# mLSTM products on full 128x128 arrays with zeroed halves, and a block inverse that starts from 8x8 blocks

## The chip, the cores and the metric

The kernel runs on one core of a Trainium2 chip. One core has a matmul engine (PE, with its weight loads listed as PEld), VectorE (DVE), ScalarE (ACT), GpSimd (POOL) and the engine that issues the transfers (SP), each with its own instruction queue, worked off in the order in which the program writes it. The metric is the time of one execution on the device, in microseconds, as the median of several runs.

## What is computed

One inference step through two layers, for a prompt of 1024 tokens and, with the same weights, for 8 sample tokens that each bring their own states. The first layer has eight heads of gated DeltaNet beside eight heads of mLSTM, the second has GLA beside retention. All matrices are float32. Two pieces of the first layer matter here, and the kernel works on both in 8 chunks of L = 128 tokens for each head.

```python
# gated DeltaNet, per head and chunk (k, q, v: L x 128; S: 128 x 128)
A = where(tri_strict, decay * (k @ k.T), 0) * beta[:, None]
rhs = beta[:, None] * (v - gam * (k @ S))
U = triangular_solve(A + eye, rhs, lower=True, unit_diagonal=True)
o = gam * (q @ S) + ((q @ k.T) * decay) @ U
S = exp(last) * S + (k * exp(last - bh)).T @ U

# mLSTM, per head and chunk (q, k: L x 64; v: L x 128; C: 64 x 128, n: 64)
num = s0[:, None] * (q @ C) + P @ v
den = s0 * (q @ n) + P.sum(-1)
h = num / maximum(abs(den), exp(-m_t))[:, None]
C = se * C + (k * we).T @ v
n = se * n + k.T @ we
```

## The kernel before

The program does not run as it is written. A recorder (class `Recorder`) collects every operation with what it reads and writes, estimates its duration, and then lists the operations of each engine in an order of its own: a backward pass gives each operation a priority by the work that depends on it, a forward pass hands each engine the ready operation of the highest priority. All instructions of the trace therefore carry the line number of the one call that replays them, L452. The planner's costs matter to the order alone. For a transfer of up to 256 KB it takes 450 ns, its bytes at 40 per ns where rows are shorter than 128 bytes, and 1400 ns until the landing: 2.7 us for 32 KB in 32-byte rows. A change in the program moves instructions everywhere, since the planner then finds another order.

Buffers that take part in the order are single slots with a name (`s_N`, `s_EM`, `s_Y`, `s_aT`, `s_vs`, `s_kd`, `s_va`, `s_mp`, `s_qs`, `s_kwe` in the trace), three each of `tmp` and `pt`, two buffers `wf` for the weights as they are loaded and two each of `whi` and `wlo`, their upper and lower parts, which ScalarE and VectorE split for the projections. A projection `pj` is 72 matmuls of 128x128 weights on 344 columns: 8 blocks of the input, 3 column groups, three products each (`whi` twice, `wlo` once). Products of the mixers go to PSUM banks A (gated DeltaNet) and B (mLSTM). Small buffers and constants show as `arena` and `base`.

`even` runs the first layer: it sets up, then alternates for each gated DeltaNet head `gdn_proj` and `gdn_mix` with a few steps of the generator `mlstm_heads`, so that projections, the inverse and both scans can be mixed by the planner.

`gdn_mix` makes `N`, the strictly lower triangular 128x128 matrix of each of the 8 chunks, stored transposed (1024 columns), and calls `inverse(N)` for the inverse of I plus that matrix. `inverse` treats the 8 chunks and the four 32x32 diagonal blocks together. It starts at pairs: four masked copies (`masked`, with the integer map `icode`) and four subtractions give `D`, the inverses of the 2x2 diagonal blocks; `Dt` is `D` transposed within the 32x32 blocks. Four doubling steps then go from 2 to 4, 8, 16 and 32. Each has 32 matmuls of 32x32 (8 chunks x 4 blocks) of N with Dt, a masked copy on VectorE, 32 matmuls of that with D, a subtraction and a transpose. The two last levels (32 to 64 to 128) use larger products and the small buffer `iw`, on which GpSimd prepares a transposed copy `Yt`. `Y` is the result. After it the scan of `gdn_mix` goes over the chunks with the state S: products with k, qg, Y, kd and aT in turn, each waiting for an update on VectorE or ScalarE.

`mlstm_mix` scans one mLSTM head. Two heads share the 128 partitions: the even head x = 0 has rows 0 to 63 (`hp`), the odd head the others. Per chunk there are three products: P with va (128x130: v, a column of ones for the normaliser, and one of padding), `qs` with the state C from the second chunk on, and `kwe` with va for the update of C. The second uses 64 rows of the array and the third writes 64 columns, by `tile_position`:

```python
self.mm(po[:, i, :], P[:, c, :], va[:, c, :], start=True, stop=C is None)
self.mm(po[:, i, :], self.qs[hp, s], C[hp, :], start=False, stop=True, tile_position=(b0, 0))
self.mm(pc[hp, 0:130], self.kwe[:, c, x, :], va[:, c, :], tile_position=(0, b0))
V.scalar_tensor_tensor(Cn[hp, :], C[hp, :], self.g_se[hp, p, c:c + 1], pc[hp, 0:130], ...)
```

Of the kernel before, what the change touches and what calls it, by code (L numbers as in the profile page):

```python
# [9 lines left out]
F32 = mybir.dt.float32  # L10
F32R = mybir.dt.float32r
AF = mybir.ActivationFunctionType
ALU = mybir.AluOpType
# [4 lines left out]
T = 1024  # L18
NS = 8
W = T + NS  # L20
# [4 lines left out]
NC = T // L  # L25
# [14 lines left out]
def host_constants():  # L40
    f = np.float32
    c = {}
# [7 lines left out]
    s, t = np.arange(L)[:, None], np.arange(L)[None, :]  # L50
# [7 lines left out]
    lm = np.zeros((32, 6, 32), f)  # L58
    ss, tt = np.arange(32)[:, None], np.arange(32)[None, :]
# [5 lines left out]

    code = np.zeros((32, 32), f)
    code[lm[:, 4, :] > 0] = 1.0
    for i, m in enumerate((2, 4, 8, 16)):
        code[lm[:, 3 - i, :].T > 0] = 2.0 + i
    c["icode"] = np.tile(code, (4, 1))  # L70

# [396 lines left out]
class Step:  # L468
# [537 lines left out]
    def even_gates(self, ps):  # L1006
        nc, a = self.nc, self.a
        dma = nc.sync.dma_start
# [79 lines left out]
        ss = self.slot("Y", [128, 6, NS], name="gss")  # L1088
# [9 lines left out]
        self.act(ss[96:104, 3, :], ss[96:104, 3, :], AF.Exp, scale=-1.0)  # L1098
        for i, r in enumerate((ss[0:8, 0, :], beta[32:40, T:W], ss[96:104, 5, :], ss[96:104, 4, :], ss[96:104, 3, :])):
            dma(self.ed[3 + i], r)  # L1100
# [193 lines left out]
    def inverse(self, N):  # L1294

        V, G = self.nc.vector, self.nc.gpsimd

        t = self.slot("EM", name="inv")
        D, Dt, At, qt = (t[:, 256 * i:256 * i + 256].rearrange("p (c t) -> p c t", c=NC) for i in range(4))

        def masked(E, out, x, i, b=slice(0, 128)):
            code = self.icode[b].unsqueeze(1).to_broadcast([b.stop - b.start, NC, 32])
            E.scalar_tensor_tensor(out, code, float(i), x, op0=ALU.is_equal, op1=ALU.mult)

        blocks = [slice(32 * j, 32 * j + 32) for j in range(4)]
        for j, b in enumerate(blocks):
            masked(V, At[b], N[b, :, b], 1, b)
        for b in blocks:
            V.tensor_tensor(D[b], self.ident[b, b].unsqueeze(1).to_broadcast([32, NC, 32]), At[b], op=ALU.subtract)
        V.transpose(Dt, D)  # L1310
        for i in range(2, 6):
            p = self.ps(None, [128, NC, 32])
            for c in range(NC):
                for j, b in enumerate(blocks):
                    self.mm(p[b, c, :], N[b, c, b], Dt[b, c, :], tile_position=(32 * j, 32 * j))
            masked(V, At, p, i)
            p = self.ps(None, [128, NC, 32])
            for c in range(NC):
                for j, b in enumerate(blocks):
                    self.mm(p[b, c, :], At[b, c, :], D[b, c, :], tile_position=(32 * j, 32 * j))  # L1320
            V.tensor_tensor(D, D, p, op=ALU.subtract)
            V.transpose(Dt, D)
# [11 lines left out]
        iw = self.small([128, 512], "iw", bufs=1)  # L1334
# [13 lines left out]
        iy = iw[:, 0:512].rearrange("p (c t) -> p c t", c=NC)  # L1348
# [119 lines left out]
    def mlstm_mix(self, h, v):  # L1468
# [33 lines left out]
        for n in (3, 3, 2):  # L1502
            po = self.ps(None, [128, 3, 130], 0)
            c0 = c
            for i in range(n):
                s = slice(128 * c, 128 * c + 128)
                self.mm(po[:, i, :], P[:, c, :], va[:, c, :], start=True, stop=C is None)
                if C is not None:
                    self.mm(po[:, i, :], self.qs[hp, s], C[hp, :], start=False, stop=True, tile_position=(b0, 0))
                pc = self.ps(i=1)  # L1510
                self.mm(pc[hp, 0:130], self.kwe[:, c, x, :], va[:, c, :], tile_position=(0, b0))
                Cn = self.small([128, 130], "C", bufs=2)
# [100 lines left out]
    def even_setup(self):  # L1613
# [3 lines left out]
        self.icode = self.const([128, 16], "icode").bitcast(mybir.dt.bfloat16)  # L1617
        code = self.slot("EM", [128, 32], name="code")
# [4 lines left out]
        self.nms = self.const([128, 2, 2, NS], "mnms")  # L1623
        self.qq = self.const([128, 2, 2, NS], "mqq")
# [480 lines left out]
    def build(self):  # L2105
        tc, nc = self.tc, self.nc
        with ExitStack() as ctx:
# [22 lines left out]
            self.rd = [dr.tile([4, QB], F32, name=f"rd{i}") for i in range(2)]  # L2130
            self.program()
# [105 lines left out]
```

## Time and profile before

| | |
|---|---|
| time before, median of 3 runs | 2360.61 us (2356.93 to 2366.92) |
| the profiled execution, its own time | 2372.93 us |
| its span | 2371.2 us |
| mean granted clock of PE | 0.979 |
| busy: PE, PEld, DVE, ACT, POOL | 97%, 89%, 60%, 32%, 22% |
| PE matmul records | 20892 |

The page describes one execution, which took 12.3 us longer than the median of the runs. Times in the rows are microseconds, except the mean of one instruction, which is in ns. A row of a group reads: line, engine, operation, output from inputs with the shapes, how often; then busy time and mean of one; then the idle time of the engine just before them and what ended it. A matmul that reads float32 shows as two records. Sizes such as 64*128 are rows times columns of the array in use. In the rows of the timeline the first number is the start, the second the length; consecutive records of one kind are put together, so the distance from one row's start to the next is what the row took of the engine.

### The profile page before, as it was taken

What the parts mean: (1) busy time and instruction counts of PE and PEld (TensorE: products, weight loads), DVE (VectorE), ACT (ScalarE), POOL (GpSimd) and SP (SyncE); (2) the same over time, 40 slices, a digit from 0 to 9 for tenths busy, and PEclk for the clock granted to TensorE, in tenths of its full rate; (3) what the DMA queues carried; (4) which work ended last, traced back from release to release, by engine and by line L of the source; (5) the groups of instructions that cost most, each with busy time, mean ns of one, the idle gap of its engine ahead of it and who ended that gap; (6) DMA issues with size and microseconds to landing.
All of it is one profiled execution on the core that took longest, in us unless ns stands there. A gap on an engine that the chain in (4) does not pass through costs nothing.

```text
span 2371.2 us, 48673 instructions
## 1 busy us (share of the span) xinstructions
PE 2297.3 (97%) x20892; PEld 2113.3 (89%) x20892; DVE 1411.5 (60%) x2700; ACT 747.3 (32%) x1374; POOL 518.8 (22%) x374
## 2 busy tenths in 40 slices
PE   7989999999999999999999999999999999998998
PEld 5878788798998989989898999999999999998998
DVE  6764645556374564755544326767877877878332
ACT  4323222232322223232233114323423423435322
POOL 4122111111202112030122003141341341343100
PEclk8999998999998999999999999999999999999999
DMA  9451533322222322222146222124224233246222
GB/s 268 117 146 53 159 102 113 108 83 71 72 55 70 91 64 78 64 88 73 56 145 173 90 63 72 46 82 127 66 87 124 63 92 119 63 126 219 81 63 90
DMA packets 250990, 232.54 MB, mean 98 GB/s; under 512 B 13595, under 2 KB 223253, under 8 KB 250766
## 3 DMA queue, kind: packets, MB, share of 16 engines
q1 hardware_dynamic: 250774, 229.42, 32.4%
q8 instruction: 164, 2.69, 0.5%
q14 instruction: 52, 0.43, 0.1%
HBM read 184.25 MB, written 45.33 MB: 97 GB/s over the span
## 4 chain that ended last, share of the span: by engine, by line
PE 86%; DVE 4%; DMA 2%; issue 1%; ACT 1%; POOL 0%; SPq 0%; POOLq 0%; DVEq 0%; ACTq 0%
PE pj L452 65%; PE A L452 14%; PE B L452 6%; DMA s_pt<-yd 1%; DVE s_h L452 1%; DVE arena L452 1%; DVE wlo L452 1%; DVE s_N L452 1%; DMA wf<-in_ev_w_in 1%; DMA s_tmp<-sd 0%; DVE s_tmp L452 0%; DVE s_vs L452 0%; DVE s_zz L452 0%; ACT whi L452 0%; DMA sd<-s_mp 0%
## 5 line engine op out<-in xcount | busy, mean ns | idle before, releaser
L452 PE MATMUL pj<-s_h,whi 128*128 128x344 f32 (+1 forms) x6024 | 1505.9, 328 | 6.3 <-DVE s_h L452 4.0
L452 PEld LDWEIGHTS pj<-s_h,whi 128*128 128x128 f32 (+1 forms) x6024 | 1049.9, 190 | 41.2 <-issue 25.0
L452 PE MATMUL pj<-s_h,wlo 128*128 128x344 f32 (+1 forms) x3024 | 986.4, 327 | 0.3 <-DVE wlo L452 0.3
L452 PEld LDWEIGHTS pj<-s_h,wlo 128*128 128x128 f32 (+1 forms) x3024 | 573.0, 190 | 20.8 <-issue 16.8
L452 DVE TENSOR_TENSOR wlo<-wf,whi 128x1024 fp32r<-128x1024 f32 (+1 forms) x144 | 199.2, 1383 | 262.1 <-ACT whi L452 248.5
L452 ACT ACTIVATE whi<-wf 128x1024 fp32r<-128x1024 f32 (+1 forms) x146 | 152.1, 1042 | 339.1 <-PE pj L452 280.8
L452 ACT ACTIVATE s_pt<-pj 128x344 f32<-128x344 f32 (+1 forms) x170 | 77.0, 453 | 340.1 <-PE pj L452 329.6
L452 POOL TENSOR_TENSOR arena<-arena,base 128x8 f32<-128x8 f32 (+5 forms) x38 | 59.5, 1566 | 471.7 <-DVE arena L452 471.5
L452 POOL TENSOR_TENSOR s_tmp<-s_EM 128x512 f32<-128x512 f32 (+1 forms) x60 | 84.2, 1426 | 157.9 <-PE A L452 62.0
L452 ACT ACTIVATE s_u<-pj 128x344 f32<-128x344 f32 x93 | 41.6, 452 | 162.5 <-PE pj L452 98.5
L452 DVE SCALAR_TENSOR_TENSOR s_pt<-s_u,base,s_pt 128x1024 f32<-128x1024 f32 x72 | 92.2, 1280 | 0.4
L452 DVE SCALAR_TENSOR_TENSOR arena<-arena,A 128x128 f32<-128x128 f32 (+1 forms) x84 | 32.8, 390 | 86.2 <-PE A L452 85.9
L452 DVE STREAM_TRANSPOSE s_kd<-s_u 32x256 f32<-32x256 f32 x128 | 55.8, 436 | 23.8 <-ACT s_u L452 21.4
L452 DVE SCALAR_TENSOR_TENSOR s_zz<-s_pt,pj 128x344 f32<-128x344 f32 x96 | 48.7, 509 | 29.1 <-ACT s_pt L452 28.2
L452 POOL TENSOR_TENSOR s_tmp<-s_tmp,arena 128x1024 f32<-128x1024 f32 (+2 forms) x26 | 44.5, 1721 | 94.6 <-PE A L452 69.5
L452 DVE SCALAR_TENSOR_TENSOR arena<-arena,B 64x130 f32<-64x130 f32 (+1 forms) x84 | 31.3, 372 | 56.8 <-PE B L452 56.2
L452 ACT ACTIVATE arena<-A,arena 128x128 f32<-128x128 f32 x64 | 23.5, 367 | 121.7 <-PE A L452 121.7
L452 ACT ACTIVATE s_tmp<-s_tmp 128x1024 f32<-128x1024 f32 (+1 forms) x44 | 46.1, 1057 | 40.6 <-POOL s_tmp L452 29.3
L452 POOL TENSOR_TENSOR s_kd<-s_kd,s_vs 128x1032 f32<-128x1032 f32 x8 | 20.2, 2524 | 172.8 <-ACT s_vs L452 172.8
L452 DVE STREAM_TRANSPOSE s_vs<-s_v 32x256 f32<-32x256 f32 x128 | 55.8, 436 | 1.9
L452 ACT ACT_TABLE_LOAD x41 | 52.6, 1283 | 5.1 <-DMA s_h<-in_x_prompt 4.4
L452 POOL MEMSET s_u<- 128x3 f32 x24 | 2.4, 100 | 233.6 <-DVE s_pt L452 233.6
(644 smaller groups left out, 3689.5 us busy)
## 6 DMA issues: line engine op xcount, KB each, us to landing
wf<-in_ev_w_in SPq DMA_DIRECT2D x64, 512.0 KB
wf<-in_od_w_in SPq DMA_DIRECT2D x48, 512.0 KB
wf<-in_ada_w SPq DMA_DIRECT2D x32, 512.0 KB
s_pt<-yd SPq DMA_DIRECT2D x24, 516.0 KB
s_tmp<-sd SPq DMA_DIRECT2D x24, 512.0 KB
yd<-s_qg SPq DMA_DIRECT2D x15, 516.0 KB
wf<-in_ev_w_out SPq DMA_DIRECT2D x14, 512.0 KB
wf<-in_od_w_out SPq DMA_DIRECT2D x14, 512.0 KB
```

The source lines that it names most:

```text
L452: op.fn(*[self.placed(x) for x in op.args], **{k: self.placed(x) for k, x in op.kw.items()})
```

## The change

Two parts. In `mlstm_mix` the product with qs uses all 128 rows: the state buffers C are now constants `mC` (two for each parity of the head) whose other half is zeroed once in `even_setup`, so the rows of the other head add nothing. The product with kwe uses both heads' 128 columns, and only the own half of the result is read.

In `inverse` the levels 1 to 8 are replaced. The four columns of 32x32 diagonal blocks of N go to DRAM (`nd`, four transfers with rows of 128 bytes); a read back puts each of the 8 x 4 x 4 = 128 diagonal blocks of 8x8 on a partition of its own (`n8`, 1024 rows of 32 bytes). Seven steps of substitution, two VectorE operations each on at most 128x7x7 elements, give the inverses `y8`. They go to DRAM (`yd`, whose other elements were zeroed at the start) and four transfers bring 32x32 blocks back as `D`. Two doubling steps remain, 8 to 16 and 16 to 32. The buffer `iw` is gone: `Yt` uses the slot of `D`, `At`, `qt` and `Dt`, so GpSimd's memset and copies for it come after the second correction's matmuls. `even_setup` gets the loads and memsets for the constants, and one small buffer gets a seventh row so that an activation doesn't write in place.

```diff
     code = np.zeros((32, 32), f)
-    code[lm[:, 4, :] > 0] = 1.0
-    for i, m in enumerate((2, 4, 8, 16)):
-        code[lm[:, 3 - i, :].T > 0] = 2.0 + i
+    for i in range(2):
+        code[lm[:, 1 - i, :].T > 0] = 1.0 + i
     c["icode"] = np.tile(code, (4, 1))
+    c["i8"] = np.tile(np.eye(8, dtype=f).reshape(1, 64), (128, 1))
...
     def inverse(self, N):
-        t = self.slot("EM", name="inv")
-        D, Dt, At, qt = (t[:, 256 * i:256 * i + 256].rearrange("p (c t) -> p c t", c=NC) for i in range(4))
...
+        nd, yd = (self.nyd[x][self.turn(x, 2)] for x in ("nd", "yd"))
+        by32 = lambda x, j: x.rearrange("(c j q) x -> c j (q x)", c=NC, j=4)[:, j, 0:1024].rearrange(
+            "c (s t) -> s c t", t=32)
+        by8 = lambda x: x[:, 0:256].rearrange("m (r t) -> m r t", t=32)[:, :, 0:8]
         blocks = [slice(32 * j, 32 * j + 32) for j in range(4)]
         for j, b in enumerate(blocks):
-            masked(V, At[b], N[b, :, b], 1, b)
-        for b in blocks:
-            V.tensor_tensor(D[b], self.ident[b, b].unsqueeze(1).to_broadcast([32, NC, 32]), At[b], op=ALU.subtract)
+            dma(by32(nd, j), N[b, :, b])
+        n8, y8, t8 = (self.const([128, 8, 8], x) for x in ("n8", "y8", "t8"))
+        dma(n8, by8(nd))
+        G.tensor_copy(y8, self.i8)
+        for s in range(7):
+            n = 7 - s
+            V.tensor_tensor(t8[:, 0:s + 1, 0:n], y8[:, 0:s + 1, s:s + 1].to_broadcast([128, s + 1, n]),
+                            n8[:, s:s + 1, s + 1:8].to_broadcast([128, s + 1, n]), op=ALU.mult)
+            V.tensor_tensor(y8[:, 0:s + 1, s + 1:8], y8[:, 0:s + 1, s + 1:8], t8[:, 0:s + 1, 0:n], op=ALU.subtract)
+        dma(by8(yd), y8)
+
+        t = self.slot("EM", name="inv")
+        D, At, qt, Dt = (t[:, 256 * i:256 * i + 256].rearrange("p (c t) -> p c t", c=NC) for i in range(4))
+        for j, b in enumerate(blocks):
+            dma(D[b], by32(yd, j))
         V.transpose(Dt, D)
-        for i in range(2, 6):
+        for i in range(1, 3):
...
-        iw = self.small([128, 512], "iw", bufs=1)
...
-        iy = iw[:, 0:512].rearrange("p (c t) -> p c t", c=NC)
+        iy = t[:, 0:512].rearrange("p (c t) -> p c t", c=NC)
...
                 if C is not None:
-                    self.mm(po[:, i, :], self.qs[hp, s], C[hp, :], start=False, stop=True, tile_position=(b0, 0))
+                    self.mm(po[:, i, :], self.qs[:, s], C, start=False, stop=True)
                 pc = self.ps(i=1)
-                self.mm(pc[hp, 0:130], self.kwe[:, c, x, :], va[:, c, :], tile_position=(0, b0))
-                Cn = self.small([128, 130], "C", bufs=2)
+                self.mm(pc[:, 0:130], self.kwe[:, c].rearrange("p x d -> p (x d)"), va[:, c, :])
+                Cn = self.mC[:, 2 * x + self.turn(f"C{x}", 2), :]
...
+        self.i8 = self.c_load("i8", [128, 8, 8])
+        zero = self.slot("aT", [128, 264], name="zero")
+        G.memset(zero, 0.0)
+        for x in self.nyd["yd"]:
+            self.nc.sync.dma_start(x, zero)
...
+        self.mC = self.const([128, 4, 130], "C")
+        for x in range(2):
+            G.memset(self.mC[64 - 64 * x:128 - 64 * x, 2 * x:2 * x + 2, :], 0.0)
...
+            self.nyd = {x: [dr.tile([128, 264], F32, name=f"{x}{i}") for i in range(2)] for x in ("nd", "yd")}
```

What the planner makes of it, at three places. A row is line, operation, output from inputs, and how often it stands there in a row.

PE at the inverse of the fifth gated DeltaNet head, before. The products of `s_EM` with `s_N` and of `s_EM` alone are the two batches of a doubling step; `s_mq` with `s_mk` belongs to mLSTM, `pj` to the projections:

```order
L452 MATMUL A_115<-s_EM_69,s_N_70 32x32 x32
L452 MATMUL B_117<-base,s_pt_83 128x128 x3
L452 MATMUL B_116<-s_mq_73,s_mk_74 128x128 x2
L452 MATMUL A_113<-s_EM_69 32x32 x32
L452 MATMUL B_116<-s_mq_73,s_mk_74 128x128 x2
L452 MATMUL B_117<-s_mq_73,s_mk_74 128x128 x3
L452 MATMUL A_114<-s_EM_69,s_N_70 32x32 x32
```

The same head after the change:

```order
L451 MATMUL A_113<-s_EM_69,s_N_70 32x32 x32
L451 MATMUL B_117<-arena,base 128x16
L451 MATMUL B_116<-s_va_75,s_mp_78 128x130
L451 MATMUL A_114<-s_EM_69 32x32 x32
L451 MATMUL B_117<-s_va_75,s_kwe_76 128x130
L451 MATMUL B_116<-s_va_75,s_mp_78 128x130
L451 MATMUL pj_110<-s_h_442,wlo_108 128x344
L451 MATMUL pj_110<-s_h_450,whi_106 128x344
L451 MATMUL pj_110<-s_h_461,whi_106 128x344
```

A batch is still 32 products, but the mLSTM products of P and va now stand between them, and there are four such batches instead of eight. Between the last product of q and k of a head and its first batch the new order has 126 to 168 projection matmuls, the old one 48 or 49.

PE where the two scans alternate, before; `arena` with `s_qs` is the product of qs with C, `s_va` with `s_kwe` the update:

```order
L452 MATMUL B_116<-arena,s_qs_77 128x130
L452 MATMUL A_115<-arena,s_k_63 128x128
L452 MATMUL A_113<-s_qg_68,arena 128x128
L452 MATMUL B_117<-s_va_75,s_kwe_76 64x130
L452 MATMUL A_115<-arena,s_Y_72 128x128
L452 MATMUL B_116<-s_va_75,s_mp_78 128x130
```

And after:

```order
L451 MATMUL A_113<-s_aT_71,arena 128x128
L451 MATMUL B_117<-s_va_75,s_kwe_76 128x130
L451 MATMUL B_116<-s_va_75,s_mp_78 128x130
L451 MATMUL A_115<-arena,s_k_63 128x128
L451 MATMUL A_113<-s_qg_68,arena 128x128
L451 MATMUL B_116<-arena,s_qs_77 128x130
L451 MATMUL B_117<-s_va_75,s_kwe_76 128x130
L451 MATMUL A_115<-arena,s_Y_72 128x128
```

The mix of the scans is much the same; kwe's output is 128x130 instead of 64x130.

SP, in the fifth head, after the change. `nd` and `yd` are the new DRAM buffers, `arena` is n8 and then y8; `sd` and `in_state_gdn` belong to the sample tokens, `wf` are weights:

```order
L451 DMA nd_129<-s_N_70 32x8x32
L451 DMA wf_104<-in_ev_w_in 128x8x128
L451 DMA nd_129<-s_N_70 32x8x32 x2
L451 DMA sd_125<-s_tmp_85 8x128
L451 DMA nd_129<-s_N_70 32x8x32
L451 DMA s_tmp_86<-sd_125 128x1024
L451 DMA s_tmp_85<-in_state_gdn 128x8x128
L451 DMA arena<-nd_129 128x8x8
L451 DMA wf_105<-in_ev_w_in 128x8x128
L451 DMA out_s_gdn<-s_tmp_87 128x8x128
L451 DMA yd_131<-arena 128x8x8
L451 DMA s_EM_69<-yd_131 32x8x32 x4
```

Before, the same stretch had the loads of `sd`, of `in_state_gdn` and of the weights alone:

```order
L452 DMA sd_125<-s_tmp_85 8x128
L452 DMA s_tmp_86<-sd_125 128x1024
L452 DMA s_tmp_85<-in_state_gdn 128x8x128
L452 DMA out_s_gdn<-s_tmp_87 128x8x128
L452 DMA wf_105<-in_ev_w_in 128x8x128
```

Ten transfers are put between them, and a weight load now stands behind the load of the 8x8 blocks, another behind the store of their inverses. On VectorE the fourteen substitution operations of that head stand between seven updates of the sample states (`s_tmp` from `s_tmp` and `s_k`, 128x128 each), and a weight split follows them:

```order
L451 SCALAR_TENSOR_TENSOR s_tmp_85<-s_tmp_87,s_k_63,s_tmp_85 128x128
L451 TENSOR_TENSOR arena<-arena 128x4x4
L451 TENSOR_TENSOR arena<-arena 128x5x3 x2
L451 TENSOR_TENSOR arena<-arena 128x6x2 x2
L451 TENSOR_TENSOR arena<-arena 128x7 x2
L451 TENSOR_TENSOR wlo_109<-wf_105,whi_107 128x1024
```

Before the change no VectorE operation in `inverse` waited for a transfer.

More of the change, by code (lines that the diff above doesn't have):

```diff
@@ L1086, in even_gates @@
         dma(self.ed[2], mp[0:8, 2, :])
-        ss = self.slot("Y", [128, 6, NS], name="gss")
+        ss = self.slot("Y", [128, 7, NS], name="gss")
         nc.gpsimd.memset(ss, 0.0)
@@ L1097, in even_gates @@
         self.act(ss[96:104, 4:6, :], ss[96:104, 4:6, :], AF.Exp)
-        self.act(ss[96:104, 3, :], ss[96:104, 3, :], AF.Exp, scale=-1.0)
-        for i, r in enumerate((ss[0:8, 0, :], beta[32:40, T:W], ss[96:104, 5, :], ss[96:104, 4, :], ss[96:104, 3, :])):
+        self.act(ss[96:104, 6, :], ss[96:104, 3, :], AF.Exp, scale=-1.0)
+        for i, r in enumerate((ss[0:8, 0, :], beta[32:40, T:W], ss[96:104, 5, :], ss[96:104, 4, :], ss[96:104, 6, :])):
             dma(self.ed[3 + i], r)
@@ L1294, in inverse @@
     def inverse(self, N):
-        V, G = self.nc.vector, self.nc.gpsimd
-        t = self.slot("EM", name="inv")
-        D, Dt, At, qt = (t[:, 256 * i:256 * i + 256].rearrange("p (c t) -> p c t", c=NC) for i in range(4))
-        def masked(E, out, x, i, b=slice(0, 128)):
-            code = self.icode[b].unsqueeze(1).to_broadcast([b.stop - b.start, NC, 32])
-            E.scalar_tensor_tensor(out, code, float(i), x, op0=ALU.is_equal, op1=ALU.mult)
+        V, G, dma = self.nc.vector, self.nc.gpsimd, self.nc.sync.dma_start
+        nd, yd = (self.nyd[x][self.turn(x, 2)] for x in ("nd", "yd"))
+        by32 = lambda x, j: x.rearrange("(c j q) x -> c j (q x)", c=NC, j=4)[:, j, 0:1024].rearrange(
+            "c (s t) -> s c t", t=32)
+        by8 = lambda x: x[:, 0:256].rearrange("m (r t) -> m r t", t=32)[:, :, 0:8]
         blocks = [slice(32 * j, 32 * j + 32) for j in range(4)]
         for j, b in enumerate(blocks):
-            masked(V, At[b], N[b, :, b], 1, b)
-        for b in blocks:
-            V.tensor_tensor(D[b], self.ident[b, b].unsqueeze(1).to_broadcast([32, NC, 32]), At[b], op=ALU.subtract)
+            dma(by32(nd, j), N[b, :, b])
[12 more added lines that the diff above has]
+            dma(D[b], by32(yd, j))
         V.transpose(Dt, D)
-        for i in range(2, 6):
+        for i in range(1, 3):
             p = self.ps(None, [128, NC, 32])
@@ L1315, in inverse @@
                     self.mm(p[b, c, :], N[b, c, b], Dt[b, c, :], tile_position=(32 * j, 32 * j))
-            masked(V, At, p, i)
+            V.scalar_tensor_tensor(At, self.icode.unsqueeze(1).to_broadcast([128, NC, 32]), float(i), p,
+                                   op0=ALU.is_equal, op1=ALU.mult)
             p = self.ps(None, [128, NC, 32])
```

## The prediction

> **What bounds the kernel now.** I read the page's busy times first, then its chain that ended last, then the windows of the first layer, then the groups on the matmul engine.
>
> ```profile
> span 2371.2 us, 48673 instructions
> ...
> PE 2297.3 (97%) x20892; PEld 2113.3 (89%) x20892; DVE 1411.5 (60%) x2700; ACT 747.3 (32%) x1374; POOL 518.8 (22%) x374
> ...
> PE 86%; DVE 4%; DMA 2%; issue 1%; ACT 1%; POOL 0%; SPq 0%; POOLq 0%; DVEq 0%; ACTq 0%
> ```
>
> PE is busy 97% of the span and is 86% of the chain that set the end; VectorE (DVE) is busy 60%. Work taken from PE shortens the kernel, and work added elsewhere costs only where PE comes to wait for it. Both edits lie in the first layer, from 160 to 1310 us:
>
> ```profile
> 160.00:1310.00 1150.00, 1121.11 (x11407) 999.90 (x11396) 623.62 (x1323) 319.36 (x650) 209.32 (x154) 0.97 0.31 91
> ```
>
> The columns are length, then busy time of PE, PEld, DVE, ACT and POOL, then granted clock, DMA share and GB/s. PE is bound here as well: 1121 of 1150 us, at a mean clock of 0.97. The groups that the change touches:
>
> ```profile
> L452 PE MATMUL A<-s_EM 32*32 32x32 f32 x2432 | 33.4, 195 | 9.3 <-issue 9.2
> L452 PE MATMUL A<-s_EM,s_N 32*32 32x32 f32 x2304 | 30.9, 194 | 6.7 <-issue 6.7
> ...
> L452 PE MATMUL B<-s_va,s_kwe 128*64 128x130 f32 x128 | 30.5, 323 | 0.2 <-DVE arena L452 0.2
> L452 PE MATMUL B<-arena,s_qs 64*128 64x130 f32 x112 | 29.1, 343 | 1.4 <-DVE arena L452 1.4
> ```
>
> An f32 matmul is two records (passes): 56 products of qs with the state and 64 updates from kwe. Records overlap, so their durations don't add; I use distances between starts.
>
> **Part A, the mLSTM products on full arrays.** A stretch where the two scans alternate (start, us):
>
> ```profile
> 749.56 0.49 PE L452 MATMUL B<-arena,s_qs 64*128 64x130 f32 x2
> 750.02 0.49 PE L452 MATMUL A<-arena,s_k 128*128 128x128 f32 x2
> 750.34 0.39 PE L452 MATMUL A<-s_qg,arena 128*128 128x128 f32 x2
> 750.66 0.43 PE L452 MATMUL B<-s_va,s_kwe 128*64 128x130 f32 x2
> 751.02 0.49 PE L452 MATMUL A<-arena,s_Y 128*128 128x128 f32 x2
> 751.35 0.39 PE L452 MATMUL B<-s_va,s_mp 128*128 128x130 f32 x2
> 751.67 0.49 PE L452 MATMUL B<-arena,s_qs 64*128 64x130 f32 x2
> ```
>
> And a run of full-array products:
>
> ```profile
> 692.24 0.39 PE L452 MATMUL A<-s_k 128*128 128x128 f32 x2
> 692.46 0.39 PE L452 MATMUL A<-s_q,s_k 128*128 128x128 f32 x2
> ...
> 692.91 0.39 PE L452 MATMUL A<-s_q,s_k 128*128 128x128 f32 x2
> ```
>
> Full products of one shape start 0.22 us apart. In the scan qs takes 0.46, kwe 0.36, and each full product beside them 0.32: the price sits at the change of shape, on both sides. From 749.56 to 751.67 six products take 2.11 us instead of 6 x 0.22 = 1.34, so 0.77 a chunk. At 56 chunks with both products that is 43 us, plus 8 first chunks with kwe alone at 0.14: 44, the upper bound. The lower bound keeps the neighbours at 0.32 and lets only their own slots go: 56 x (0.46-0.22) + 64 x (0.36-0.22) = 22. I take **-40**, near the upper one, because in the quoted stretch every full product borders a changed shape; a tenth is left for chunks whose neighbours are something else. That full arrays make the passes themselves no longer is seen at mp: the same 130 columns on the full array, 0.32 in the same place.
>
> The Trainium skill, "TensorEngine Tiling (Array Packing)", section "The Problem", counts a contraction of 64 or less among the cases where the full array is wasted, and the change goes the other way. Its section "Key Properties" also says that a switch of tiling mode drains the array. The trace bears out the second (0.46 against 0.22) and not the first. By the first alone this part would give 0.
>
> **Part B, the inverse's matmuls.** One batch is 32 products of 32x32, 64 records:
>
> ```profile
> 714.41 0.32 PE L452 MATMUL pj<-s_h,wlo 128*128 128x344 f32 x1
> 714.57 0.32 PE L452 MATMUL pj<-s_h,whi 128*128 128x344 f32 x1
> 714.82 0.75 PE L452 MATMUL A<-s_EM,s_N 32*32 32x32 f32 x64
> 715.50 0.42 PE L452 MATMUL pj<-s_h,whi 128*128 128x344 f32 x1
> 715.76 0.32 PE L452 MATMUL pj<-s_h,wlo 128*128 128x344 f32 x1
> ```
>
> From 714.57 to 715.76 lie two projection matmuls at 0.16 (714.41 to 714.57) and one batch: 1.19 - 0.32 = 0.87. The doubling steps go from four to two, two batches each, in eight heads: 32 batches, **-28**. By the batch's own slot alone (714.82 to 715.50) it is 0.68 x 32 = 22, the lower bound; a doubling batch next to other changed shapes might give up to 34.
>
> **Part C, idle inside these batches.** The two groups of 32x32 products sit idle 9.3 + 6.7 = 16 us, nearly all "issue". Ten batches a head use these arrays, four go: 16 x 0.4, **-6** (bounds 0 and -10).
>
> **Part D, what is added.** The start of the inverse becomes a chain through DRAM: four stores of N's diagonal blocks, a load as 8x8 blocks, 14 small DVE operations, a store, four loads, a transpose. Rows nearest to its steps:
>
> ```profile
> L452 DVE SCALAR_TENSOR_TENSOR s_N<-A,arena,s_EM x64: 335/343/351, 145.3 to 1127.4; 128x128 f32<-128x128 f32 x64
> ...
> L452 DVE STREAM_TRANSPOSE s_EM<-s_EM x40: 429/445/448, 157.1 to 1154.4; 128x256 f32<-128x256 f32 x40
> ...
> L452 DVE SCALAR_TENSOR_TENSOR s_EM<-arena,s_N x32: 361/421/1767, 152.4 to 1131.9; 32x256 f32<-32x256 bf16 x32
> L452 DVE TENSOR_TENSOR s_EM<-base,s_EM x32: 405/416/422, 155.1 to 1133.8; 32x256 f32<-32x256 f32 x32
> ```
>
> ```profile
> L452 DVE TENSOR_TENSOR arena<-arena 128x8 f32<-128x8 f32 x56 | 9.8, 175 | 7.7 <-ACT arena L452 6.8
> ```
>
> ```profile
> 1265.73 12.36 DMA s_pt<-yd
> ...
> 2194.67 1.61 DMA rd<-s_aT
> 2196.33 3.79 DMA s_aT<-rd
> ```
>
> ```profile
> 746.80 0.33 SPq L452 DMA_DIRECT2D yd<-arena  x1
> ```
>
> N's eight products take 8 x 0.34 = 2.7, about 4 with the pieces that feed them. Four stores: 4 x 0.33 to issue and 1.61 until the last has landed, 2.9. The load: 0.33 + 3.79 = 4.1. The 14 operations: 14 x 0.175 = 2.5, with seven state updates of 128x128 for the sample tokens set between them at 0.34, 4.9. Store 1.9, four loads 1.3 + 3.8 = 5.1, transpose 0.4. Together **about 23 us**. These legs have short rows that no row shows: I take them from the small store (1.61) and the read-back (3.79); the ends are nothing and the 12.36 us that one read-back of 516 KB held up the chain.
>
> The cover: before, 9.65 us pass from the last product of q and k (692.91) to the first batch:
>
> ```profile
> 702.31 0.32 PE L452 MATMUL pj<-s_h,wlo 128*128 128x344 f32 x1
> 702.56 0.75 PE L452 MATMUL A<-s_EM,s_N 32*32 32x32 f32 x64
> ```
>
> The new order puts 126 to 168 projection matmuls there where 48 stood: at 0.16, 20 to 27 us, and some 5 us of scan products. So 25 us or more cover 23, just.
>
> DVE itself gains per head: it loses eight operations of 0.42 and two doubling steps' three of 0.42 to 0.45, and adds 14 x 0.175: 3.4 + 2.6 - 2.5 = 3.5 us less, which its 60% hides. SP issues ten more DMAs a head, 3.3 us; weight loads queue behind those that wait, but two buffers of 72 matmuls (11.5 us each) stand ahead. The reuse of EM moves GpSimd's steps behind the second correction:
>
> ```profile
> L452 POOL COPY arena<-s_EM 32x256 f32<-32x256 f32 x16 | 6.5, 409 | 192.8 <-DVE s_EM L452 192.4
> ...
> L452 POOL MEMSET arena<- 32x256 f32 x8 | 2.4, 302 | 24.3 <-PE A L452 24.3
> ```
>
> 0.3 + 2 x 0.41 = 1.1 us later; the projection matmuls between those batches hide it, else it costs 9 us over eight heads. The planner allows about 2.7 us for a small leg; a leg of 3.79 is 1.1 later, and behind the DVE operation that waits for it stands a weight split (wlo), and then the transpose, for which PE waits: 8 x 1.1, **+10** with the extra setup (bounds 0 and the rivals).
>
> **Sum**, against the profiled execution's own 2372.9 us: 2372.9 - 40 - 28 - 6 + 10 = 2309. That execution lies 12.3 above the median of the runs (2360.6), so **2297 us**.
>
> **Rivals.**
>
> Slow legs: each leg takes what the longer loads do in the chain:
>
> ```profile
> 357.81 6.93 DMA s_tmp<-sd
> ```
>
> That is 4.2 us past the planner's 2.7, and after a stop PE runs at half clock for a while:
>
> ```profile
> 709.88 0.59 PE L452 MATMUL A<-s_EM 32*32 32x32 f32 x46 [1.54 <-issue]
> ...
> 713.01 0.49 PE L452 MATMUL pj<-s_h,wlo 128*128 128x344 f32 x1
> 713.30 0.49 PE L452 MATMUL pj<-s_h,whi 128*128 128x344 f32 x1
> ```
>
> Starts 0.29 apart instead of 0.16, from 710.4 to 713.9: 1.6 us lost. So 8 x (4.2 + 1.6) = 46 in place of 10, **2333**. For it: cover and chain are near equal, and the load of the 8x8 blocks is issued behind two loads of 512 KB. The Trainium skill, "DMA: Bandwidth & Descriptors", section "Specifications", says that below 512 B a transfer does a read-modify-write and misses line rate, and the rows here are 32 and 128 B; no run here shows its price. Against it: a leg moves only 32 to 128 KB.
>
> No gain from shape: the scan's products are slow for their 130 columns or for waits on DVE, and stay so. Part A falls away: **2337**. For it: the groups of qs and kwe wait for DVE at times. Against it: the k products, with 128 columns, slow down beside them and run at 0.22 elsewhere.
>
> The chain of the recurrence: PE gets through a chunk faster than DVE updates the state, and half of A comes back as waits: **2317**.
>
> More than counted: stops of 1.54 us like the one above lie in the batches that go, about 16 x 0.4 / 1.54 = 4, each with 1.6 us of half clock, and A gives all 44, B 34: **2280**.
>
> **Slower**: the first substitution operation stands at the head of DVE until the 8x8 blocks have landed; behind it stand the other substitution steps and the next weight split, and PE stops at the first product of that split. With a leg of 12.36, 9.7 past the plan: 8 x (9.7 + 1.6) = 90, so 2373 - 74 + 90 - 12 = **2377**. It outweighs the gain of 74 from 9.2 a head, a leg of 10.3 us; a whole projection's matmuls ahead of that split (11.5 us) would take its edge off. For it: each engine takes its work in the written order. Against it: that row is one wait of 516 KB after a layer's end.
>
> **How the numbers follow.** Forecast 0.46, slow legs 0.19, no gain from shape 0.08, recurrence 0.10, more than counted 0.12, slower 0.05. About 0.5% (12 us) is what a measurement can tell from no change: faster means under 2349. Of the slow legs and the lost A a quarter could end within it, and a little of the rest: faster 0.89, same 0.06, slower 0.05. The range reaches from 2262 (all upper bounds, some more half clock gone) to 2340, past slow legs and the lost A.
>
> **What would show it.** In the scan, products of qs and kwe start 0.22 apart and their neighbours too; 32x32 records fall from 4736 to 2688; no idle on PE before the first batch; the clock of 160 to 1310 us is no lower than 0.97. Idle of PE before the first batch or before wlo's matmuls, ending after a small load lands, would make the prediction wrong; so would starts of 0.32 that stay.

## The result and the profile after

| | before | after |
|---|---|---|
| median | 2358.77 us (4 runs, 2355.56 to 2366.92) | 2287.93 us (4 runs, 2282.23 to 2290.45) |
| ratio, 95% interval | | 0.9691, 0.966 to 0.9723 |
| profiled execution: own time, span | 2372.93, 2371.2 us | 2289.05, 2287.0 us |
| mean granted clock of PE | 0.979 | 0.987 |

The changed kernel takes 3.1% less time. The forecast was 2297 us with a range of 2262 to 2340. The page of the changed kernel, busy times and then shares of the chain that ended last:

```profile
span 2287.0 us, 44726 instructions
...
PE 2221.4 (97%) x18844; PEld 2070.0 (91%) x18844; DVE 1382.8 (60%) x2700; ACT 747.7 (33%) x1374; POOL 527.7 (23%) x385
...
PE 88%; DMA 4%; DVE 4%; issue 1%; ACT 1%; POOL 1%; SPq 1%; POOLq 0%; DVEq 0%; ACTq 0%
```

PE still sets the time: 97% busy, with 2048 records fewer, the 32 batches of 64. The first layer, in the windows view of the changed kernel (columns as before):

```profile
160.00:1228.00 1068.00, 1053.67 (x9535) 967.79 (x9534) 594.25 (x1338) 322.70 (x653) 213.01 (x162) 0.99 0.36 102
```

It takes 1068 us where it took 1150: 82 of the 84 us between the two profiled executions. PE's busy time there falls by 67 us, its idle time from 29 to 14, and its clock rises from 0.97 to 0.99. What PE waited for in the first layer, in the waits view, engine and releaser, then us in all, times and the longest, first of before:

```profile
PE A L452 <- issue: 15.9, 10, 3.0
```

and of the changed kernel:

```profile
PE A L451 <- issue: 1.9, 3, 0.8
...
PE A L451 <- DVE s_EM L451: 1.0, 2, 0.9
```

The stops inside the 32x32 batches are nearly gone, and the new wait, for the transpose behind the way through DRAM, is 1 us over all eight heads. The array shapes in the group rows of the changed kernel:

```profile
L451 PE MATMUL B<-s_va,s_kwe 128*128 128x130 f32 x128 | 26.0, 284 | 0.1
...
L451 PE MATMUL A<-s_EM 32*32 32x32 f32 x1408 | 19.9, 194 | 0.1
L451 PE MATMUL B<-arena,s_qs 128*128 128x130 f32 x112 | 22.9, 286 | 0.4 <-DVE arena L451 0.4
```

qs took 343 ns a record and kwe 323; both are at 285 now, on the full array.

**How the runs are read below.** A difference of medians mixes three things: the time that PE works, the time that it stands, and the time that it loses at half clock. They can be told apart from numbers of one profiled execution: span minus busy time is what PE stands; span x (1 - mean clock) is what it loses (the clock of stopped stretches counted in); busy time minus that is the **net work**, PE's work at full clock. For before: 2371.2 - 2297.3 = 73.9, 2371.2 x 0.021 = 49.8, net 2247.5. After: 65.6, 29.7, net 2191.7. So of 84 us, 56 are work that is gone, and 28 are stops and half clock. The clock has three places, so the last two columns below are good to about 1 us. They also describe one execution each: over 40 executions of the kernel before, the clock ran from 0.973 to 0.989 and the span from 2349.9 to 2385.1 us, with the same order.

| kernel | median us | ratio to before (95%) | span | PE stands | lost to clock | net work |
|---|---|---|---|---|---|---|
| before | 2358.8 to 2365.3, in five measurements | | 2371.2 | 73.9 | 49.8 | 2247.5 |
| before, planner 185 ns | 2362.9 | 0.9986 (0.996 to 1.0012) | 2352.5 | 73.3 | 37.6 | 2241.6 |
| before, planner overlap | 2353.7 | 0.9958 (0.9923 to 0.9992) | 2351.1 | 75.0 | 28.2 | 2247.9 |
| slot reuse alone | 2341.4 | 0.9908 (0.9881 to 0.9934) | 2337.7 | 61.2 | 28.1 | 2248.4 |
| slot reuse, qs full | 2335.9 | 0.9874 (0.9847 to 0.9902) | 2333.7 | 67.1 | 35.0 | 2231.6 |
| slot reuse, qs and kwe full | 2323.8 | 0.9828 (0.9805 to 0.9851) | 2325.8 | 75.8 | 32.6 | 2217.4 |
| new inverse alone | 2308.9 | 0.9768 (0.9743 to 0.9794) | 2309.6 | 69.7 | 23.1 | 2216.8 |
| changed kernel | 2287.9 | 0.9691 (0.966 to 0.9723) | 2287.0 | 65.6 | 29.7 | 2191.7 |
| changed, planner 185 ns | 2292.3 | 0.9697 (0.9663 to 0.9732) | 2288.1 | 67.4 | 36.6 | 2184.1 |
| changed, planner overlap | 2277.2 | 0.9641 (0.9607 to 0.9675) | 2275.7 | 61.8 | 22.8 | 2191.1 |
| changed, one unseen copy | 2284.6 | 0.9674 (0.9643 to 0.9705) | 2281.7 | 64.0 | 27.4 | 2190.3 |
| changed, one planned copy | 2283.0 | 0.9669 (0.9638 to 0.9701) | 2281.0 | 69.1 | 22.8 | 2189.1 |
| changed, three unseen copies | 2338.8 | 0.9893 (0.9838 to 0.9949) | 2338.7 | 98.7 | 53.8 | 2186.2 |
| substitution to 16x16 | 2259.5 | 0.9578 (0.9534 to 0.9621) | 2257.3 | 57.9 | 20.3 | 2179.1 |

### The profile page after: what moved, and what is told of

Read it like the earlier page. It is cut to its first block, busy times and chain, and to the rows that moved or that the text cites. A ratio compares the mean times of both kernels' runs of the same rounds, so it can differ in the third digit from the quotient of the medians.

```text
span 2287.0 us, 44726 instructions
## 1 busy us (share of the span) xinstructions
PE 2221.4 (97%) x18844; PEld 2070.0 (91%) x18844; DVE 1382.8 (60%) x2700; ACT 747.7 (33%) x1374; POOL 527.7 (23%) x385
## 4 chain that ended last, share of the span: by engine, by line
PE 88%; DMA 4%; DVE 4%; issue 1%; ACT 1%; POOL 1%; SPq 1%; POOLq 0%; DVEq 0%; ACTq 0%
PE pj L451 68%; PE A L451 14%; PE B L451 6%; DMA wf<-in_ev_w_in 1%; SPq L451 1%; DMA s_aT<-rd 0%; DVE s_h L451 0%; DMA s_h<-in_x_prompt 0%; DVE arena L451 0%; DVE s_N L451 0%; DMA s_pt<-yd 0%; DVE s_pt L451 0%; DMA ed<-s_Y 0%; DMA s_mp<-gd 0%; DVE s_mp L451 0%
## 5 line engine op out<-in xcount | busy, mean ns | idle before, releaser
L451 DVE TENSOR_TENSOR wlo<-wf,whi 128x1024 fp32r<-128x1024 f32 (+1 forms) x144 | 192.9, 1340 | 291.2 <-ACT whi L451 272.3
L451 ACT ACTIVATE whi<-wf 128x1024 fp32r<-128x1024 f32 (+2 forms) x146 | 152.1, 1043 | 374.9 <-PE pj L451 330.3
L451 POOL TENSOR_TENSOR arena<-arena,base 128x8 f32<-128x8 f32 (+5 forms) x38 | 64.4, 1697 | 377.8 <-DVE arena L451 377.1
L451 POOL TENSOR_TENSOR s_tmp<-s_EM 128x512 f32<-128x512 f32 (+1 forms) x60 | 88.5, 1493 | 156.2 <-PE A L451 69.1
```

The costliest lines, as they stand in the source:

```text
L451: op.fn(*[self.placed(x) for x in op.args], **{k: self.placed(x) for k, x in op.kw.items()})
```

## The experiments

**The parts alone.** First only the reuse of the EM slot, in the old inverse; without it the arena has no room for the zeroed states, so the next two kernels contain it too.

```diff
-        D, Dt, At, qt = (t[:, 256 * i:256 * i + 256].rearrange("p (c t) -> p c t", c=NC) for i in range(4))
+        D, At, qt, Dt = (t[:, 256 * i:256 * i + 256].rearrange("p (c t) -> p c t", c=NC) for i in range(4))
...
-        iw = self.small([128, 512], "iw", bufs=1)
...
-        iy = iw[:, 0:512].rearrange("p (c t) -> p c t", c=NC)
+        iy = t[:, 0:512].rearrange("p (c t) -> p c t", c=NC)
```

> Only the reuse of the EM slot in place of the small buffer iw, with the old inverse and the old mLSTM products. Theory (the gain comes from PE work that goes): between 0 and +9 us against the kernel before, since GpSimd's memset and two copies, 1.1 us a head, move behind the second correction and projection matmuls cover them. Rival (any other order that the planner finds moves the time by as much as the change did): a difference of over 12 us in either direction.

Measured: 2341.4, 23 us faster than before measured beside it, which the forecast had not seen and which the rival here had: more than 12 us. Its net work is that of before (2248.4 against 2247.5): all of the gain lies in stops and half clock, 89.3 us instead of 123.7. The controls further down say what that means.

Then the product with qs on full rows (the first pair of lines), and both products; both kernels take C from `mC`:

```diff
-                    self.mm(po[:, i, :], self.qs[hp, s], C[hp, :], start=False, stop=True, tile_position=(b0, 0))
+                    self.mm(po[:, i, :], self.qs[:, s], C, start=False, stop=True)
...
-                self.mm(pc[hp, 0:130], self.kwe[:, c, x, :], va[:, c, :], tile_position=(0, b0))
+                self.mm(pc[:, 0:130], self.kwe[:, c].rearrange("p x d -> p (x d)"), va[:, c, :])
```

> The slot reuse and the product of qs with C on full rows with zeroed halves; kwe keeps its 64 columns. Theory (the price lies at the change of array shape, on both sides of a product): 13 us from its own slots (56 x 0.24) plus up to 56 x 2 x 0.1 = 11 from the neighbours, so -13 to -24 against the run with the slot reuse alone; in the timeline qs starts 0.22 before its neighbour unless kwe follows. Rival (130 columns or waits on VectorE are what makes the product slow): 0, and qs still takes 0.4 or more.

Measured: net work falls by 16.8 us, the median by 5.5, since stops and half clock come to 102 us again. The mechanism is seen in the timeline of the kernel with qs full and kwe on 64 columns (start, length in us):

```profile
740.08 0.39 PE L452 MATMUL B<-arena,s_qs 128*128 128x130 f32 x2
740.30 0.49 PE L452 MATMUL A<-arena,s_k 128*128 128x128 f32 x2
740.63 0.39 PE L452 MATMUL A<-s_qg,arena 128*128 128x128 f32 x2
740.85 0.39 PE L452 MATMUL B<-s_va,s_mp 128*128 128x130 f32 x2
741.08 0.39 PE L452 MATMUL B<-arena,s_qs 128*128 128x130 f32 x2
741.30 0.42 PE L452 MATMUL A<-arena,s_Y 128*128 128x128 f32 x2
741.66 0.44 PE L452 MATMUL B<-s_va,s_kwe 128*64 128x130 f32 x2
742.02 0.43 PE L452 MATMUL pj<-s_h,whi 128*128 128x344 f32 x1
```

qs now starts 0.22 before its neighbour, at the same 130 columns, and kwe still takes 0.36: the shape it was, not the columns. Nor are 64 rows slow in themselves. In the kernel before, five products of mLSTM's q and k on 64 rows stand behind one another:

```profile
705.04 1.38 PE L452 MATMUL B<-s_mq,s_mk 64*128 64x128 f32 x10
```

Single records of this row, the first apart, start 0.11 us apart, so a product takes 0.22 here too: the price lies at the change of shape. But the product with k (740.30) takes 0.33 here too, with full products on both sides. The forecast had put such 0.1 us down to a neighbour's shape.

> The slot reuse and both mLSTM products on full arrays, the old inverse. Theory (change of shape): -40 against the run with the slot reuse alone (22 to 44), about 20 more than with qs alone. Rival (columns or waits): 0. Rival (the scan's recurrence takes back half): -20, with idle time of PE released by VectorE's state updates in the scan. The clock should stay near that of before, since all batches of 32x32 products with their stops remain.

Measured: net work 31.0 us less than with the slot reuse alone, within the bounds of 22 to 44 and under the 40 taken; the median falls by 17.7, because this order stands and loses 108 us, 19 more. The rival of 0 misses the net work. Net work can't judge the recurrence, whose loss would be standing time, and the median alone is close to its -20. The waits view of the first layer can: waits for VectorE's updates in the two scans come to 6.4 us here,

```profile
PE B L452 <- DVE arena L452: 3.8, 3, 2.2
...
PE A L452 <- DVE arena L452: 2.6, 5, 1.3
```

where the slot reuse alone has 0.3:

```profile
PE B L452 <- DVE arena L452: 0.3, 2, 0.2
```

So the recurrence takes back some 6 us in this order and not half; in the changed kernel these waits are 1.5 us.

The new inverse with the old mLSTM products (the lines of `mlstm_mix` and `mC` undone in the changed kernel):

> The new inverse alone, mLSTM products as before. Theory as predicted: -28 for 32 batches, -6 for idle time, +10 for the way through DRAM: -24 against before. Theory after the result (the way through DRAM is covered, and stops at half clock go with the batches): -34 to -50, with PE's idle time on issue at 2 to 5 us instead of 16 and a mean clock 0.005 or more above the kernel before. If the two parts are independent, this and the run with both mLSTM products sum to the whole change, about -70.

Measured: 56 us faster than before, 6 more than the upper end expected; against the slot reuse alone, which it also contains, 32.5 by medians and 31.6 in net work. PE's stops on issue in the first layer, 15.9 us before, are 2.0, and the clock is 0.990. The two parts are nearly independent: in net work, mLSTM gives 31.0 beside the old inverse and 25.1 beside the new (2216.8 - 2191.7), the inverse 31.6 beside the old products and 25.7 beside the new. Together 56.7 (2248.4 - 2191.7), not 62.6. The difference lies at the neighbours of the mLSTM products: the mean slot of aT, for one, is 0.25 us with the slot reuse alone and already 0.19 with the new inverse alone, so there was less to win. By medians, 41 us for both products and 56 for the inverse make 97; both contain the slot reuse, and with its 23 counted once they make 74, near the whole change.

**Controls: another order of the same program.** One line of the planner's figures is changed, so that the operations are the same and their order differs.

```diff
-    DRAIN = 170.0
+    DRAIN = 185.0
```

> A control: the kernel before with the planner's figure for the time from a matmul to its reader at 185 ns instead of 170. The program computes the same with the same operations and buffers; only the order on the engines differs. Theory (the 22 us of the slot reuse are owed to the new order, in which fewer stops of PE lead to half clock): this differs from before by 8 to 25 us, with its mean clock away from 0.979, and most of the difference is clock. Rival (the slot reuse has a gain of its own): within 6 us of before, clock 0.977 to 0.982.

```diff
-    OVERLAP = dict(vector=80.0, scalar=98.0, gpsimd=42.0)
+    OVERLAP = dict(vector=75.0, scalar=95.0, gpsimd=42.0)
```

> A second control: the kernel before with the planner's overlap of VectorE and ScalarE operations at 75 and 95 ns instead of 80 and 98. The same two theories: order alone, 8 to 25 us away from before, in step with the clock lost; or within 6 us of before.

> The changed kernel with the planner's 185 ns. Theory (with four of ten batches of 32x32 products gone, the first layer has few stops left whatever the order): within 8 us of the changed kernel, 2280 to 2296. Rival (the changed kernel has a lucky order): 10 to 25 us slower, with more clock lost in the first layer.

> The changed kernel with the planner's overlaps at 75 and 95 ns. The same: within 8 us of the changed kernel if the gain does not hang on one order, 10 to 25 us slower if it does.

Measured: the two orders of before lie 2 and 12 us under it, the two of the changed kernel 4 over and 11 under; the last is more than the 8 us expected, and on the fast side, which neither theory had. The first control can't be told from before (its interval includes 1), as the rival had it, though its profiled execution had a clock of 0.984. So the order alone is worth up to some 10 us. Net work moves by 8 us at most; in the profiled executions stops and half clock run from 103 to 124 us in the three orders of before and from 85 to 104 in the three of the changed kernel.

The 23 us of the slot reuse are more than these controls show. The three kernels that have it with the old inverse share a low loss at half clock over all their executions, 29 to 32 us, where before has 43 and the two controls 41 and 33. Whether that is a gain of the reuse or an order that the three inherit is not settled here.

In the mean of the profiled executions, before and its two controls stand and lose 113 us, the three with slot reuse and the old inverse 100, and the six with the new one at 8x8 and up to one copy 93. For the whole change the medians say much the same: of 70.8 us, 56 are net work, which leaves **about 15**. So some 15 of the 28 us belong to the change, slot reuse included, and the rest is that the profiled execution of before was at the bad end.

**The way through DRAM.** One more copy on its chain, which the planner counts as nothing, so that the order stays:

```diff
+        op.unseen = queue == "sync" and writes[0].name.startswith("n2")
...
-        dma(n8, by8(nd))
+        n2 = self.nyd["n2"][self.turn("n2", 2)]
+        rows = lambda x: x.rearrange("(m q) x -> m (q x)", q=4)[:, 0:1024]
+        dma(rows(n2), rows(nd))
+        dma(n8, by8(n2))
```

> The changed kernel with one more copy on the chain of the inverse, DRAM to DRAM, 128 KB, between the store of N's blocks and the load of the 8x8 blocks. The planner counts it as nothing, so the order on PE and VectorE stays that of the changed kernel but for a few rows. Theory (the cover is laid out by the planner to be just enough, as the 0.16 us that PE waited for the transpose in one head suggests): two to four us more in each of eight heads, so 16 to 40 us slower with the half clock that follows stops, and idle time of PE put down to VectorE's transpose or to the small load. Rival (the cover has room to spare): within 6 us of the changed kernel.

Measured: 2284.6, 3 us under the changed kernel; the rival holds. The copy is there: on SP's queue it is issued at 661.45, and the load that waits for it at 664.78, 3.3 us later. That load then lands sooner: over the eight heads the blocks are there 5.7 us after the first issue in the mean, where the load alone takes 3.5, so the copy makes them 2.3 us late.

```profile
661.45 0.53 SPq L456 DMA_DIRECT2D n<-nd  x1
664.78 0.39 SPq L456 DMA_DIRECT2D arena<-n  x1
```

VectorE waits for it, too. Groups on VectorE with the idle time before them, the changed kernel, then with one copy, then with three:

```profile
L451 DVE TENSOR_TENSOR arena<-arena 128x7 f32<-128x7 f32 x32 | 5.4, 167 | 5.5 <-DMA arena<-nd 4.9
```

```profile
L456 DVE TENSOR_TENSOR arena<-arena 128x7 f32<-128x7 f32 x32 | 5.4, 168 | 16.9 <-DMA arena<-n 16.3
```

```profile
L456 DVE STREAM_TRANSPOSE s_EM<-s_EM 128x256 f32<-128x256 f32 x24 | 10.7, 444 | 33.7 <-DMA s_EM<-yd 33.2
...
L456 DVE TENSOR_TENSOR arena<-arena 128x7 f32<-128x7 f32 x32 | 5.4, 168 | 53.9 <-DMA arena<-n 53.3
```

With one copy VectorE stands 16.3 us instead of 4.9 at the first substitution operation: 11 more, of 8 x 2.3 = 18. In the head at 650 us of the changed kernel, for one, the blocks have landed at 667.08, and VectorE, busy with other work, comes to them at 670.48. PE hardly notices: it waits 2.8 us for the transpose instead of 1.0, and stands no longer in all. There is cover to spare.

> The same copy, this time counted by the planner with its usual figures. Theory (projections that don't depend on the inverse can be drawn ahead as far as needed): within 8 us of the changed kernel. Rival (the supply of projections ahead of the first batch is used up): as slow as with the copy that the planner doesn't see.

Measured: 2283.0, as expected; counted by the planner, it costs nothing either.

Three unseen copies in a row:

> Three copies on the chain instead of one, all unseen by the planner: with about 3.3 us each, some 10 us in each head, what the prediction's slower case puts on this place (a leg of 12.4 us). The order on PE and VectorE is that of the run with one unseen copy. Prediction's slower case: VectorE stands at the first substitution operation, the weight split behind it is late, PE stops for nearly all of it: 8 x (9.7 + 1.6) = 90 us, so about 2375. Theory after the run with one copy (2 us more of VectorE's waiting a head cost PE less than a quarter of it, since a projection's matmuls of 11.5 us and the time between the last N and the blocks' need lie ahead): 3 to 6 us a head of stops plus half clock, 25 to 65 slower than the changed kernel. If there are 10 us of room: within 8 us of it.

Measured: 2338.8, 51 us slower than the changed kernel, within the 25 to 65 expected after the run with one copy. In one head the copies take from 554.26 to 562.63, 8.4 us, and over the eight heads the blocks are there 10.7 us after the first issue, 7.2 later than without copies:

```profile
554.26 0.50 SPq L456 DMA_DIRECT2D n<-nd  x1
557.90 2.77 SPq L456 DMA_DIRECT2D n<-n  x2
562.63 0.39 SPq L456 DMA_DIRECT2D arena<-n  x1
```

VectorE stands 53.3 us there, and PE for the transpose (waits view):

```profile
PE A L456 <- DVE s_EM L456: 16.0, 3, 6.3
```

PE stands 98.7 us instead of 65.6 and loses 53.8 to the clock instead of 29.7: 4.1 + 3.0 us a head. Of the 7.2, some 4 come through as standing time in the mean, so the room is estimated at **about 3 us a head**; past it each microsecond costs about one and a half with the clock. It is uneven: the stops at the transpose lie in three heads only. The first product of the weight split (`wlo`), where the prediction's slower case saw PE stop, costs it 0.6 us, once; the other long waits are elsewhere. Even this stays 1% under before.

**One level more by substitution.** Blocks of 16x16, with n, y and the temporary in the EM slot, and a single doubling step:

```diff
-        for s in range(7):
-            n = 7 - s
...
+        n8, y8, t8 = (t[0:64, 256 * i:256 * i + 256].rearrange("p (r t) -> p r t", t=16) for i in (1, 2, 3))
+        dma(n8, by16(nd))
...
+        for s in range(15):
+            n = 15 - s
...
-        for i in range(1, 3):
+        for i in range(2, 3):
```

> The substitution goes up to 16x16 blocks (64 of them on 64 partitions, 30 operations instead of 14, in the free parts of the EM slot), and one doubling step remains. Theory (net work of PE and its stops go with the batches): 16 batches at 0.87 = -14 us against the changed kernel, a little more with stops, and the longer chain (16 operations more at 0.2 to 0.3, 3 to 5 us a head) is covered by the planner: -10 to -18. Rival (the chain no longer finds cover, or VectorE's weight splits come late): 0 to +15.

Measured: 2259.5 us, 28 under the changed kernel and 4.2% under before: faster than expected. Net work falls by 12.6 us, near the 14 for 16 batches; stops and half clock by 17, of which the scatter of orders (10 either way) may be a good part. The batches in the first layer, in the group rows of this kernel:

```profile
L451 PE MATMUL A<-s_EM 32*32 32x32 f32 x896 | 13.3, 193 | 0.3 <-ACT s_EM L451 0.3
L451 PE MATMUL A<-s_EM,s_N 32*32 32x32 f32 x768 | 11.6, 193 | 0.9 <-DVE s_EM L451 0.9
```

Of the 16 us on "issue" that stood in these groups before none is left.

## Why the prediction was right, and where its terms were not

The time came out 9 us under the forecast, and the direction is beyond doubt. But the sum held in part by luck, because wrong terms cancelled: part A was too large by some 12 us, against which part D charged 10 that did not come and part C took 9 too few.

**Part A, -40: over-sized; -31 beside the old inverse, -25 beside the new.** That the price lay at the change of shape is shown: qs alone took 16.8 us of net work out, and its slot is 0.22 at 130 columns. The step that failed is "near the upper one, because in the quoted stretch every full product borders a changed shape": one stretch was taken for all chunks. Over all chunks of the kernel before, 62% of the products with k and 59% of those with qg already started 0.24 us or less before the next. From the slot reuse alone to both products full, the mean slot of qs goes from 0.42 to 0.25 and that of kwe from 0.37 to 0.24, 18 us where the sum had 22; the neighbours give 12 where it had 18. Beside the new inverse it is 17 and 6. The medians fall by only 17.7 and 21.0 us. The scan in the changed kernel, all on the full array:

```profile
700.11 0.39 PE L451 MATMUL B<-s_va,s_mp 128*128 128x130 f32 x2
700.34 0.39 PE L451 MATMUL B<-arena,s_qs 128*128 128x130 f32 x2
700.74 0.49 PE L451 MATMUL A<-arena,s_kd 128*128 128x128 f32 x2
701.06 0.39 PE L451 MATMUL A<-s_aT,arena 128*128 128x128 f32 x2
701.28 0.39 PE L451 MATMUL B<-s_va,s_kwe 128*128 128x130 f32 x2
701.51 0.39 PE L451 MATMUL B<-s_va,s_mp 128*128 128x130 f32 x2
701.73 0.42 PE L451 MATMUL A<-arena,s_k 128*128 128x128 f32 x2
701.99 0.39 PE L451 MATMUL A<-s_qg,arena 128*128 128x128 f32 x2
702.21 0.40 PE L451 MATMUL B<-arena,s_qs 128*128 128x130 f32 x2
702.45 0.39 PE L451 MATMUL B<-s_va,s_kwe 128*128 128x130 f32 x2
```

aT, kwe, mp and kwe start 0.22 or 0.23 before the next, but kd, which multiplies the U just written by ScalarE, still takes 0.32 (700.74 to 701.06), and the qs at 700.34 takes 0.40, since kd waits for that U until 700.69. kd's median slot over all chunks is 0.32 or 0.33 in all 14 kernels, with full neighbours or half ones. For a product whose operand has just been made the 0.1 us were not the neighbour's shape.

**Part B, -28: right.** 31.6 and 25.7 us of net work, by the pairs above, within its bounds of 22 and 34.

**Part C, -6, and the stops: under-sized.** "Four of ten go" was a count by batches. Measured, the idle time on issue in the first layer went from 15.9 to 1.9 us, and that is not one order's luck: it is 10 to 16 us in the six kernels with the old inverse and 1 to 3 in the six with the new one at 8x8 and up to one copy. With it goes half clock behind stops, which the sum left out and the fourth rival had at 6 us. Stops and half clock together make about 15 us. A stop in a batch and its echo in the kernel before, by windows of 3.4 us (PE's busy time and granted clock are the second and third numbers):

```profile
707.20:710.60 3.40, 1.86 (x69) 1.00 0.03 9
710.60:714.00 3.40, 3.40 (x13) 0.50 0.55 158
714.00:717.40 3.40, 3.40 (x140) 1.00 0.38 112
```

A stretch in which PE stood 1.54 of 3.4 us is followed by one at half clock. The Trainium skill, "TensorE: Matmul & The Clock Gate", section "What's actually happening", gives a free-running window of 3413 ns, which fits; its table speaks of an idle window before the clock falls, and here a window that was 55% busy was enough. It is not always enough. With the first layers of all 14 kernels cut into windows of this length, in step with the half-clock stretches, the windows at full clock divide so: of 27 in which PE was busy for less than 40%, all are followed by half clock; of 112 between 40% and 80%, 28; of 4471 above, none.

**Part D, +10: not there.** The chain of the head at 650 us runs from the last product of q and k (653.26) to the first batch (681.55), 28.3 us against 23 in the forecast. Most legs were priced well: the load of the 8x8 blocks lands 3.2 us after its issue (4.1 in the forecast), the store of the inverses 2.1 (1.9), the four loads 4.8 (5.1). The 5 us more lie in one store of N's blocks that took 5.4 and in VectorE's other work before the substitution. PE waits 0.16 us at its end:

```profile
681.55 0.75 PE L451 MATMUL A<-s_EM,s_N 32*32 32x32 f32 x64 [0.16 <-DVE s_EM L451]
```

```profile
670.48 0.16 DVE L451 TENSOR_TENSOR arena<-arena 128x7 f32<-128x7 f32 x1
...
671.34 2.66 DVE L451 TENSOR_TENSOR arena<-arena 128x7 f32<-128x7 f32 x13
...
681.05 0.45 DVE L451 STREAM_TRANSPOSE s_EM<-s_EM 128x256 f32<-128x256 f32 x1 [0.44 <-DMA s_EM<-yd]
```

The 14 operations take 2.8 us of VectorE in all. What failed is "a leg of 3.79 is 1.1 later" as a cost to PE: VectorE did wait for the blocks (4.9 us over eight heads), but PE had cover past that, as the unseen copy shows. The same runs weigh the rivals. The "slow legs" put this one at 2.7 + 4.2 = 6.9 us: 5.7 cost nothing, and by the estimate of 3 us of room past the 3.5 measured, 6.9 would have cost little. The slower case was right that a late leg stops PE, but its price was too high and its place wrong: a leg of 10.7 us, 8.0 past the plan, comes to 8 x (8.0 + 1.6) = 77 by its formula and cost 51, because the formula left no room, and PE stopped at the transpose and hardly at the weight split.

**The slot reuse** was costed at 0 to 9 us in the GpSimd term. Nothing in net work or waits shows that cost. It came out 23 us faster, all of it in stops and half clock, and no term of the sum had that.

**No gain from shape** is refuted by the run with qs alone; **the recurrence** takes back no half of part A, though some 6 us in one order, and it holds part of the 0.1 us. **More than counted**: half clock and stops did go, to the size of about 15 us by the medians and 28 in the two profiled executions.

## What to carry to other kernels

Where single half-array products stood among full ones on a busy matmul engine, the change of shape cost more than the rows and columns saved, and padding with zeros was cheaper; half-array products in a row paid nothing. Price such a product and its neighbours over all chunks and not from one stretch, since a fresh operand gives the same 0.1 us. And where a planner or scheduler writes the order, compare a change with one or two other orders of the same program before reading 10 us into it: span minus busy time, the clock lost and the net work tell which part is the change.

## What the hardware showed that was not expected

Stops of PE inside dense runs of 32x32 products, for which the waits view names no releaser ("issue"), were 15.9 us in the first layer before, ten stops of up to 3.0 us; in the kernel with 16x16 blocks, which has a third of these records (1664 of 4736), the groups show none. The traces point to what they wait for. The page of the kernel before lists a queue of its own for instructions (packets, MB, share of the DMA engines):

```profile
q8 instruction: 164, 2.69, 0.5%
```

Its 164 packets have 16384 bytes each, one for about 255 of PE's matmuls and weight loads. All 77 stops of 0.3 us or more on "issue" in the first layers of the 14 kernels end 1.2 to 1.7 us after a packet of this queue has landed; of points taken at random in the first layer of before 4% lie so. The stop at 709.88 follows a packet from 707.43 to 708.50. Within a kernel, consecutive stops lie a multiple of 128 matmul records apart, to within 13. Past the start of a kernel two of these packets never begin less than 3.2 us apart, while a batch of 64 records took 0.87. So PE works off its instructions faster than they come when several batches stand close together; fewer batches, with longer matmuls between them, let the packets keep up. No run here changed the packets themselves, so this is read from the traces and not tried. And the echo of the stops on the clock comes in pieces that are not in proportion: in the windows of the changed kernel between 350 and 750 us the clock reads 1.00 twice, in those of before 0.96 and 0.95.

```profile
350.00:550.00 200.00, 194.74 (x1755) 0.96 0.33 98
550.00:750.00 200.00, 193.63 (x2337) 0.95 0.22 67
```

```profile
350.00:550.00 200.00, 199.53 (x1648) 1.00 0.37 103
550.00:750.00 200.00, 198.83 (x1986) 1.00 0.30 86
```

At 200 us each, 0.04 and 0.05 are 18 us lost, behind 11.6 us of standing.
